# Half-size products for values and gate: the norm factor at the end, its chain in one piece, the squares in other places

## The chip, the core and the metric

The kernel runs on one core of a Trainium2 chip. The core's engines work side by side, each through its own queue, in order: TensorE (PE) does matmuls into PSUM banks, VectorE (DVE) and ScalarE (ACT) do elementwise work, GpSimd (POOL) does some more of it, and SyncE (SP) issues DMAs. Semaphores make one engine wait for another. The metric is the device time of one execution in microseconds (us). The profile shows one execution, from its first to its last instruction (the span).

## What is computed

```python
h = rmsnorm(x, g_mix)                       # x is (1, 512, 1024) float32
z = h @ w_in
q_r, k_r, v_r, gt_r, q_f, k_f, v_f, f_f, a_r, a_f = split_cols(z)
y_r = W_ro( silu(gt_r) * GroupNorm( Retention(rot(q_r), rot(k_r), v_r) ) )
y_f = W_fo( ForgettingAttention(rmsnorm(q_f), rmsnorm(k_f), v_f, log_sigmoid(f_f + b_forget)) )
x = x + W_out( sigmoid(a_r) * y_r + sigmoid(a_f) * y_f )
x = x + SwiGLU(rmsnorm(x))
```

`rmsnorm` multiplies each token's row by `rsqrt(mean(x*x) + 1e-6)`, one number per token, and each column by a gain. The kernel puts the gain into `x` before the products. The number per token, `rstd1`, can be multiplied in behind a product, because a product works on each token's row alone. This case is about the place where that is done for `v_r` (the values) and `gt_r` (the gate).

## The kernel before

**Precision.** Every float32 operand of a matmul is split in two: a leading part (a cast, on ACT) and the remainder (a subtraction, on DVE). `split_raw` (lines 150 to 156) does so for a weight tile of 128 x 1024, `x_sum` (lines 318 to 329) for a sum of blocks of `x`. Three matmuls stand for one product. Weight parts have three buffers (`WB`), so a cast waits until PE has used the tile three places before it.

**Values and gate.** Both have 512 columns. For pairs of blocks the kernel doesn't do eight block products but seven, of sums of blocks (lines 361 to 405). This text calls them products 1 to 7, in order of their calls of `products`:

| product | weights | `x` | banks | adds to |
|---|---|---|---|---|
| 1 | `B11` | `A11` | `x_` | new |
| 2 | `t1` = `B11 + B12` | `s1` = `A21 - A22` | `z_` | new |
| 3 | `B11 + B12 + B22` | `s2` = `s1 - A11` | `x_` | product 1 |
| 4 | `B21` | `A12` | `y_` | new |
| 5 | `t3` = `B12 + B22` | `s3` = `A11 - A21` | `x_` | product 3 |
| 6 | `B22` | `s4` = `s2 + A12` | `z_` | product 2 |
| 7 | `B11 + B12 + B22 + B21` | `A22` | `x_` | product 5 |

Each is 4 blocks of rows x 2 banks x 3 = 24 matmuls of 512 columns. The weight blocks are added in place, so an addition to `B11` waits until the sum before it is split. Product 7 goes bank by bank, the others change banks at every block. Where a product adds to banks that another one filled, the partial sum is first copied out of PSUM into a quarter of `us`. The values `vr` and the gate `gs` come from these quarters and the last banks.

**The norm factor.** Four squares on ACT, with `accum_out`, give the sums `ss1` from `xs`, the token-major copy of `x`, which a DMA brings (line 226). `rsqrt` (lines 109 to 124) makes `rstd1` from them by twelve small instructions on DVE, each depending on the one before. `us` lies in the space of `xs`. The copies out of PSUM (lines 374, 379, 383, 391), the evacuation of the earlier product of `q_r` and `k_r` from the banks `sc` and `tp` to `rz` (lines 375 and 376) and the last steps of `vr` and `gs` all multiply by `rstd1`. Product 4 writes to the `sc` banks.

**Behind the products.** `broadcast_cols` (lines 240 to 250, called in line 410) turns `rstd1` into rows for the gates: with a tile `wide` it makes one broadcast copy on DVE and then four turns on PE, without it four small products into `rb`, which has two buffers, each with a turn. GpSimd rotates `q_r` and `k_r` (`ret_rotate`); its first instruction is made to wait for the last remainder of `t3` (`t3_low`). Then pieces of the retention alternate on PE with the steps of other products, which `fill(RF[...])` places by their cost in us (lines 661 to 686); one step of `w_qf` has three matmuls. The last step for each token tile evacuates `qf` and writes `fz` (line 548) from the same bank. `ret_norm` takes statistics (`bn_stats`, line 501).

**Order.** A planner places each engine's instructions in the order of the code as they come ready. PE's order is pinned between the lines that set `pinned[0]`. `after(a, b)` adds an edge: `a` comes behind `b` on their engine. The norm chain is put behind `t1`'s last remainder (`behind=t1_low`, line 371).

Of the kernel before, what the change touches and what calls it, by code (L numbers as in the profile page):

```python
# [9 lines left out]
F32 = mybir.dt.float32  # L10
F32R = mybir.dt.float32r
I32 = mybir.dt.int32
BF16 = mybir.dt.bfloat16
AF = mybir.ActivationFunctionType
ALU = mybir.AluOpType
AX = mybir.AxisListType

P = 128
D = 1024
S = 512  # L20
NT = S // P
NK = D // P
RH, RDK, RDV = 4, 64, 128
FH, FD = 8, 64
# [10 lines left out]
C_BF = C_GFFN + NK  # L35
# [18 lines left out]
def block_kernel(ctx: ExitStack, tc, x, xT, c_early, c_tab, c_late, w_qf, w_tok, w_vg, w_a, w_y, w_o, w_gu, w_dn, w_dh, out):  # L54
    nc = tc.nc
    PS = bass.MemoryType.PSUM
    tt, ts, stt = nc.vector.tensor_tensor, nc.vector.tensor_scalar, nc.vector.scalar_tensor_tensor
    act = nc.scalar.activation
    pinned = [False, None]

    def after(ins, prev):

        tc.add_manual_dep(ins.ins, prev.ins.name, mybir.DependencyInfo(mybir.DependencyClass.NoSync, mybir.DependencyReason.DATA), reason="order")
# [27 lines left out]
    def bank(tag):  # L91
        return ps.tile([P, 512], F32, name=tag, tag=tag, bufs={"acc": 4, "sc": 2, "tp": 2}[tag])
# [6 lines left out]
    r1 = cst.tile([P, S], F32, name="r1")  # L99
# [9 lines left out]
    def rsqrt(dst, ss, inv_n, shape, nm, pool=None, behind=None):  # L109

        v = (pool or sm).tile(shape, F32, name=nm + "v", tag=nm + "v", bufs=1 if pool else 2)
        yi = (pool or sm).tile(shape, I32, name=nm + "y", tag=nm + "y", bufs=1 if pool else 2)
        a = (pool or sm).tile(shape, F32, name=nm + "a", tag=nm + "a", bufs=1 if pool else 2)
        y = yi.bitcast(F32)
        first = ts(out=v, in0=ss, scalar1=inv_n, scalar2=EPS, op0=ALU.mult, op1=ALU.add)
        if behind is not None:
            after(first, behind)
        ts(out=yi, in0=v.bitcast(I32), scalar1=1, scalar2=None, op0=ALU.logical_shift_right)
        ts(out=yi, in0=yi, scalar1=-1.0, scalar2=float(0x5F3759DF), op0=ALU.mult, op1=ALU.add)
        for i in range(3):  # L120
            stt(out=a, in0=y, scalar=-0.5, in1=y, op0=ALU.mult, op1=ALU.mult)
            tt(out=a, in0=a, in1=v, op=ALU.mult)
            last = stt(out=dst if i == 2 else y, in0=a, scalar=1.5, in1=y, op0=ALU.add, op1=ALU.mult)
        return last
# [6 lines left out]
    WU, WP = 1056, 1152  # L131
    RAW, WB, SG, PT, PR, TB, CBUF = 2, 3, 12, 2, 4, 2, 2
    PREP = [3, 5]
    RF, CF, PF, SF, LAG = (5.32, 4.64, 5.6, 4.6, 11.2), (3.0, 2.0, 2.26, 4.0), 5.9, (0.63, 0.83, 1.57, 1.4), 3
    VF = 1.8

    raw_pools, part_pools, turns = [wp] * RAW, [wp] * WB, [0, 0]
# [163 lines left out]
    def evac_to(dst, func):  # L301
        def f(t, c, acc):
            act(out=dst[:, t, :], in_=acc, func=func, scale=rstd1[:, t:t + 1])
        return f
# [13 lines left out]
    def x_sum(n, p, q, op, behind=None):  # L318

        for i in range(2):  # L320
            to = sums[:, n, 2 * i:2 * i + 2, :]
            p_, q_ = (to if b is None else xv[i][:, :, b[0], b[1]:b[1] + HS] for b in (p, q))
            one = tt(out=to, in0=p_, in1=q_, op=op)
            if behind is not None:
                after(one, behind)
        h = bp.tile([P, 4, HS], F32R, name="sh", tag="sh", bufs=2)
        l = bp.tile([P, 4, HS], F32R, name="sl", tag="sl", bufs=2)
        split_to_parts(sums[:, n], h, l)
        return lambda j, tp: tuple(f[:, j, tp * P:(tp + 1) * P] for f in (h, l))
# [5 lines left out]
    def x_block(b):  # L335
        return lambda j, tp: tuple(f[:, 2 * j + b[0], b[1] + tp * P:b[1] + (tp + 1) * P] for f in (xh, xl))

    def halves_of(block, add=None, behind=None):

        parts = []  # L340
        for v in range(2):
            if add is not None:
                one = tt(out=block[:, v, :], in0=block[:, v, :], in1=add[:, v, :], op=ALU.add)
                if behind is not None:
                    after(one, behind)
            parts.append(split_raw(block[:, v, :]))
        return parts

    def products(os, parts, stat, new, by_bank=False):
        steps = [(j, tp) for j in range(4) for tp in range(2)]  # L350
        for j, tp in sorted(steps, key=lambda s: s[1]) if by_bank else steps:
            h, l = parts[j // 2]
            cs = slice(j % 2 * 512, j % 2 * 512 + 512)
            sh, sl = stat(j, tp)
            for n, (a, b) in enumerate(((sh, h), (sl, h), (sh, l))):
                mm(os[tp], lhsT=a, rhs=b[:, cs], start=new and j + n == 0, stop=j == 3 and n == 2, skip_group_check=not new)

    def scaled(o, bank_, t):
        act(out=o, in_=bank_, func=AF.Copy, scale=rstd1[:, t:t + 1])

    z_ = [bank("acc") for _ in range(2)]
    x_ = [bank("acc") for _ in range(2)]
    pinned[0] = True
    b11 = halves_of(B11)
    products(x_, b11, x_block(A11), True)
    s1, t1 = x_sum(0, A21, A22, ALU.subtract), halves_of(B11, B12, split_raw.last[1])
    for t in range(NT):
        junk = ftok.tile([P, D], BF16, name="junk", tag="sq", bufs=1)
        after(act(out=junk, in_=xs[t // 2][:, t % 2, :], func=AF.Square, accum_out=ss1[:, t:t + 1]), split_raw.last[0])
    t1_low = split_raw.last[1]  # L370
    r_last = rsqrt(rstd1, ss1, 1.0 / D, [P, NT], "n1", behind=t1_low)
    us = [ftok.tile([P, 4, 512], F32, name="u", tag=n) for n in ("qf", "kf")]
    for tp in range(2):
        scaled(us[tp][:, 0, :], x_[tp], tp)
    for t in range(NT):
        evac_to(rz, AF.Copy)(t, 0, accs[t])
    products(z_, t1, s1, True)
    for tp in range(2):
        scaled(us[tp][:, 3, :], z_[tp], tp + 2)
    s2 = x_sum(0, None, A11, ALU.subtract)  # L380
    products(x_, halves_of(B11, B22), s2, False)
    for tp in range(2):
        scaled(us[tp][:, 1, :], x_[tp], tp)
    y_ = [bank("sc") for _ in range(2)]
    products(y_, halves_of(B21), x_block(A12), True)
    s3 = x_sum(1, A11, A21, ALU.subtract, t1_low)
    t3 = halves_of(B12, B22, t1_low)
    t3_low = split_raw.last[1]
    products(x_, t3, s3, False)
    for tp in range(2):  # L390
        scaled(us[tp][:, 2, :], x_[tp], tp + 2)
    s4 = x_sum(0, None, A12, ALU.add, r_last)
    vr = rtok.tile([P, NT, 512], F32, name="vr", tag="rtok0")
    gs = rtok.tile([P, NT, 512], F32, name="gs", tag="rtok1")
    for tp in range(2):
        stt(out=vr[:, tp, :], in0=y_[tp], scalar=rstd1[:, tp:tp + 1], in1=us[tp][:, 0, :], op0=ALU.mult, op1=ALU.add)
    products(z_, halves_of(B22), s4, False)
    for tp in range(2):
        tt(out=gs[:, tp + 2, :], in0=us[tp][:, 3, :], in1=us[tp][:, 2, :], op=ALU.subtract)
        act(out=gs[:, tp + 2, :], in_=gs[:, tp + 2, :], func=AF.Silu)  # L400
        stt(out=gs[:, tp, :], in0=z_[tp], scalar=rstd1[:, tp:tp + 1], in1=us[tp][:, 1, :], op0=ALU.mult, op1=ALU.subtract)
        act(out=gs[:, tp, :], in_=gs[:, tp, :], func=AF.Silu)
    products(x_, halves_of(B11, B21, r_last), x_block(A22), False, by_bank=True)
    for tp in range(2):
        scaled(vr[:, tp + 2, :], x_[tp], tp + 2)
    pinned[0] = False
    bp.release()
    orp = tc.alloc_tile_pool(name="orp", bufs=1, side="right")
    sgp = tc.alloc_tile_pool(name="sgp", bufs=1, side="right")
    broadcast_cols(rstd1, r1)  # L410


    orh = orp.tile([P, RH, S], F32R, name="orh")
# [5 lines left out]
    xiT = cl[:, C_XI:C_LATE].rearrange("p (a q) -> p a q", a=2)  # L419
    gp = nc.gpsimd  # L420
    ret = [{} for _ in range(NT)]

    def ret_rotate(t):
        z5 = rz[:, t, :].rearrange("p (a h s d) -> p a h s d", a=2, h=RH, s=2)
# [69 lines left out]
    def ret_norm(t):  # L494
        o = ret[t]["o"]
        o = [o[h % 2][:, (h // 2) * P:(h // 2 + 1) * P] for h in range(RH)]
        mv = sm.tile([P, RH, 2], F32, name="mv", tag="mv")
        bs = sm.tile([P, RH, 6], F32, name="bs", tag="bs")
        r4 = sm.tile([P, RH], F32, name="r4", tag="r4")
        for h in range(RH):  # L500
            nc.vector.bn_stats(out=bs[:, h, :], in_=o[h])
            nc.vector.bn_aggr(out=mv[:, h, :], in_=bs[:, h, :])  # L502
        rsqrt(r4, mv[:, :, 1], 1.0, [P, RH], "n4")
        og = rwk.tile([P, 512], F32, name="og", tag="og")
        for h in range(RH):
            hs = slice(h * P, (h + 1) * P)
            ts(out=og[:, hs], in0=o[h], scalar1=mv[:, h, 0:1], scalar2=r4[:, h:h + 1], op0=ALU.subtract, op1=ALU.mult)
        ret[t].update(og=og)
# [35 lines left out]
    def evac_qf(t, c, acc):  # L544
        sc = rstd1[:, t:t + 1]
        act(out=qf[:, t, c * 256:c * 256 + 256], in_=acc[:, 0:256], func=AF.Copy, scale=sc)
        if c:
            stt(out=fz[:, t, :], in0=acc[:, 256:264], scalar=sc, in1=ce[:, C_BF:C_BF + FH], op0=ALU.mult, op1=ALU.add)
            qnorm(t)

    def evac_kf(t, c, acc):
# [7 lines left out]
        return cb  # L559

    ra, rb = slice(0, FD), slice(FD, P)
    fox = {}

    def fox_prep(a, part):

# [615 lines left out]
```

## Time and profile before

| what | value |
|---|---|
| median of three runs | 723.43 us (723.15 to 724.76) |
| the profiled execution | 722.19 us |
| its span | 720.4 us |
| mean granted clock of PE | 0.995 |
| DVE busy, 33.86 to 44.63 us | 10.56 of 10.77 us |
| DVE busy, 49.12 to 62.30 us | 7.79 of 13.18 us |
| GpSimd busy, 57.69 to 75.41 us | 16.93 of 17.72 us |

The page gives each engine's busy time and its share of the span. A line of the list of waits has the waiting engine, its tile and line, the releaser, the us in total, how often, and the longest. A row of the timeline has start, duration, engine, line and operation; what stands in square brackets is the idle time of the engine before it, with the releaser. A grouped row has the busy time, the mean duration in ns, and the idle time before. A row of the windows has the window, its length, the busy time with the number of instructions, the clock granted to PE (1.00 is full), the share of the DMA engines and GB/s. A row of the DMA issues ends with KB and the us from issue to landing.

### The profile page before, as it was taken

To read this page: it belongs to the slowest core of one execution; us is meant where nothing else is said; L and a number is where in the kernel's file an instruction comes from. 1 tells how busy PE (TensorE), PEld (TensorE's weight loads), DVE (VectorE), ACT (ScalarE), POOL (GpSimd) and SP (SyncE) were. 2 spreads that over 40 slices of the span, in tenths; PEclk is the share of its full clock that TensorE was granted. 3 is DMA by queue.
4 is the path that set the end of the run, shared out by engine and by line. 5 is a ranking of instruction groups with operands and counts; after the bars stand their busy time and mean duration, and the time that the engine had idled before them with its cause. 6 is when DMAs were issued, how large, how long until landed. Compare 5 with 4: busy or idle time off the path is not lost.

```text
span 720.4 us, 10869 instructions
## 1 busy us (share of the span) xinstructions
PE 703.4 (98%) x4283; PEld 618.4 (86%) x4283; DVE 541.6 (75%) x876; ACT 363.5 (50%) x556; POOL 75.1 (10%) x90
## 2 busy tenths in 40 slices
PE   8969899999999999999999999999999999999998
PEld 6848888888877767888888999999999998888998
DVE  6978558756687786637868788899889998844684
ACT  6666343432576666324644655555655555532251
POOL 0007823011021130000220000000000000000000
PEclk9989999999999999999999999999999999999999
DMA  8900312222322221236503133323332214343112
GB/s 280 417 8 1 119 59 89 88 64 97 112 81 74 89 74 58 89 112 232 211 0 117 60 117 118 102 75 118 117 117 68 110 38 139 117 164 99 62 70 76
DMA packets 19907, 76.33 MB, mean 106 GB/s; under 512 B 2312, under 2 KB 2952, under 8 KB 16656
## 3 DMA queue, kind: packets, MB, share of 16 engines
q1 hardware_dynamic: 19712, 75.62, 31.0%
q8 instruction: 33, 0.54, 0.3%
q14 instruction: 18, 0.15, 0.1%
q10 hardware_dynamic: 144, 0.02, 0.0%
HBM read 73.52 MB, written 2.11 MB: 105 GB/s over the span
## 4 chain that ended last, share of the span: by engine, by line
PE 88%; DVE 5%; ACT 3%; issue 2%; POOL 1%; DMA 1%; SPq 0%; ACTq 0%; DVEq 0%
PE acc L72 55%; PE sc L72 27%; PE tp L72 5%; PE tp L75 1%; DVE pr L607 1%; DVE wl L155 1%; POOL cb L599 1%; ACT wh L154 1%; ACT pr L609 1%; ACT tk L574 1%; DMA raw<-in_w_tok_dram 1%; ACT tk L573 1%; DVE kl L576 1%; DVE pr L611 0%; ACT tq L584 0%
## 5 line engine op out<-in xcount | busy, mean ns | idle before, releaser
L154 ACT CAST wh<-raw 128x1024 fp32r<-128x1024 f32 (+1 forms) x44 | 46.2, 1050 | 93.9 <-PE acc L72 84.7
L72 PE MATMUL sc<-xfh,cl 128*128 128x256 f32 x288 | 83.2, 289 | 0.0
L72 PE MATMUL sc<-xfh,ch 128*128 128x256 f32 x288 | 81.6, 283 | 0.0
L72 PE MATMUL sc<-xfl,ch 128*128 128x256 f32 x288 | 81.4, 283 | 0.0
L155 DVE TENSOR_TENSOR wl<-raw,wh 128x1024 fp32r<-128x1024 f32 (+1 forms) x44 | 56.3, 1280 | 26.1 <-ACT wh L154 26.1
L848 DVE TENSOR_TENSOR cl<-t,ch 128x1024 fp32r<-128x1024 f32 x48 | 58.7, 1222 | 13.7 <-ACT ch L848 13.6
L72 PE MATMUL acc<-xfh,ah 128*128 128x256 f32 (+1 forms) x216 | 63.9, 296 | 0.0
L72 PE MATMUL acc<-xfh,al 128*128 128x256 f32 (+1 forms) x216 | 63.7, 295 | 0.0
L72 PE MATMUL acc<-xfl,ah 128*128 128x256 f32 (+1 forms) x216 | 63.7, 295 | 0.0
L848 ACT CAST ch<-t 128x1024 fp32r<-128x1024 f32 x48 | 50.5, 1052 | 12.8 <-PE tp L72 8.0
L72 PEld LDWEIGHTS sc<-xfh,cl 128*128 128x128 f32 x288 | 55.0, 191 | 0.8 <-DVE cl L848 0.2
L72 PEld LDWEIGHTS sc<-xfh,ch 128*128 128x128 f32 x288 | 55.1, 191 | 0.3 <-ACT u L909 0.2
L72 PEld LDWEIGHTS sc<-xfl,ch 128*128 128x128 f32 x288 | 55.1, 191 | 0.0
L72 PE MATMUL acc<-xh,wh 128*128 128x512 f32 x128 | 52.4, 410 | 0.0
L72 PE MATMUL acc<-wh,xh 128*128 128x512 f32 (+2 forms) x144 | 50.5, 351 | 0.8 <-DVE mv L502 0.8
L72 PE MATMUL acc<-xh,wl 128*128 128x512 f32 x128 | 50.1, 392 | 0.0
L72 PE MATMUL acc<-xl,wh 128*128 128x512 f32 x128 | 49.9, 390 | 0.0
L72 PE MATMUL acc<-wl,xh 128*128 128x512 f32 (+2 forms) x144 | 49.4, 343 | 0.0
L72 PE MATMUL acc<-wh,xl 128*128 128x512 f32 (+2 forms) x144 | 49.4, 343 | 0.0
L848 DVE TENSOR_TENSOR al<-raw,ah 128x1536 fp32r<-128x1536 f32 x24 | 42.2, 1757 | 6.9 <-ACT ah L848 6.9
L72 PEld LDWEIGHTS acc<-xfh,al 128*128 128x128 f32 x216 | 41.3, 191 | 1.0
L72 PEld LDWEIGHTS acc<-xfl,ah 128*128 128x128 f32 x216 | 41.3, 191 | 0.9
(313 smaller groups left out, 1916.2 us busy)
## 6 DMA issues: line engine op xcount, KB each, us to landing
raw<-in_w_gu_dram SPq DMA_DIRECT2D x21, 1024.0 KB, 4.7
raw<-in_w_a_dram SPq DMA_DIRECT2D x16, 512.0 KB, 3.5
t<-in_w_dn_dram SPq DMA_DIRECT2D x14, 512.0 KB, 3.6
blk<-in_w_vg_dram SPq DMA_DIRECT2D x8, 512.0 KB, 10.0
raw<-in_w_tok_dram SPq DMA_DIRECT2D x8, 512.0 KB, 3.5
raw<-in_w_y_dram SPq DMA_DIRECT2D x8, 512.0 KB, 3.5
raw<-in_w_o_dram SPq DMA_DIRECT2D x8, 512.0 KB, 3.6
raw<-in_w_dh_dram SPq DMA_DIRECT2D x4, 1024.0 KB, 4.9
```

The lines of the kernel that those rows point to most:

```text
L72: in_order(nc.tensor.matmul(o, **kw))
L75: in_order(nc.tensor.transpose(out=o, in_=src, identity=ident))
L154: split_raw.last = (nc.scalar.copy(out=h[:, :width], in_=raw[:, :width]), tt(out=l[:, :width], in0=raw[:, :width], in1=f32(h)[:, :width], ...
L155: tt(out=l[:, :width], in0=raw[:, :width], in1=f32(h)[:, :width], op=ALU.subtract))
L573: act(out=tk[e][r], in_=pk[r], func=AF.Copy, scale=gk[r])
L574: act(out=tk[e][o], in_=pk[r], func=AF.Copy, scale=gk[r])
L576: stt(out=kl[e][r], in0=pk[r], scalar=gk[r], in1=f32(tk[e])[r], op0=ALU.mult, op1=ALU.subtract)
L599: gp.tensor_tensor(out=cb[:, qs], in0=cb[:, qs], in1=mask, op=ALU.add)
L607: nc.vector.tensor_tensor_reduce(out=pr[:, :n], in0=cb[:, :n], in1=sc[:, :n], scale=-1.0, scalar=3e38, op0=ALU.add, op1=ALU.min, accum_out=nm)
L609: fox["last"] = act(out=pr[:, :n], in_=pr[:, :n], func=AF.Exp, scale=-1.0, bias=nm, accum_out=rs)
L848: split_to.last = nc.scalar.copy(out=h, in_=src), tt(out=l, in0=src, in1=f32(h), op=ALU.subtract)
```

## The change

It does five things.

1. The copies out of PSUM don't multiply by `rstd1` any more. `vr` is scaled in place on ACT behind its last addition, and `gs` in its Silu.
2. The four squares move: two behind the cast of `B11`'s second half, two between the casts of `t1`'s halves.
3. The norm chain comes behind `t1`'s last remainder as before, and the remainders of the third weight sum and its second addition come behind the chain. The block additions of `t1` and of product 3 are written out half by half. The sums for `s3` and `t3` come behind the remainders of product 3's weights.
4. `broadcast_cols` gets a tile `wide`.
5. `RF[0]` grows from 5.32 to 5.72, and `bn_stats` comes behind the last `fz` traced by then.

```diff
-    RF, CF, PF, SF, LAG = (5.32, 4.64, 5.6, 4.6, 11.2), (3.0, 2.0, 2.26, 4.0), 5.9, (0.63, 0.83, 1.57, 1.4), 3
+    RF, CF, PF, SF, LAG = (5.72, 4.64, 5.6, 4.6, 11.2), (3.0, 2.0, 2.26, 4.0), 5.9, (0.63, 0.83, 1.57, 1.4), 3
...
+    def squares(t, behind):
+        junk = ftok.tile([P, D], BF16, name="junk", tag="sq", bufs=1)
+        one = act(out=junk, in_=xs[t // 2][:, t % 2, :], func=AF.Square, accum_out=ss1[:, t:t + 1])
+        after(one, behind)
+        return one
+
+    def add_to(block, v, other, behind=None):
+        one = tt(out=block[:, v, :], in0=block[:, v, :], in1=other[:, v, :], op=ALU.add)
+        if behind is not None:
+            after(one, behind)
+
     z_ = [bank("acc") for _ in range(2)]
     x_ = [bank("acc") for _ in range(2)]
     pinned[0] = True
-    b11 = halves_of(B11)
-    products(x_, b11, x_block(A11), True)
-    s1, t1 = x_sum(0, A21, A22, ALU.subtract), halves_of(B11, B12, split_raw.last[1])
-    for t in range(NT):
-        junk = ftok.tile([P, D], BF16, name="junk", tag="sq", bufs=1)
-        after(act(out=junk, in_=xs[t // 2][:, t % 2, :], func=AF.Square, accum_out=ss1[:, t:t + 1]), split_raw.last[0])
+    products(x_, halves_of(B11), x_block(A11), True)
+    s1 = x_sum(0, A21, A22, ALU.subtract)
+    sq = squares(1, squares(0, split_raw.last[0]))
+    b11_low = split_raw.last[1]
+    add_to(B11, 0, B12)
+    add_to(B11, 1, B12, b11_low)
+    t1 = [split_raw(B11[:, 0, :])]
+    after(split_raw.last[0], sq)
+    sq = squares(3, squares(2, split_raw.last[0]))
+    t1.append(split_raw(B11[:, 1, :]))
+    after(split_raw.last[0], sq)
     t1_low = split_raw.last[1]
-    r_last = rsqrt(rstd1, ss1, 1.0 / D, [P, NT], "n1", behind=t1_low)
     us = [ftok.tile([P, 4, 512], F32, name="u", tag=n) for n in ("qf", "kf")]
     for tp in range(2):
-        scaled(us[tp][:, 0, :], x_[tp], tp)
+        nc.scalar.copy(out=us[tp][:, 0, :], in_=x_[tp])
+    products(z_, t1, s1, True)
+    s2 = x_sum(0, None, A11, ALU.subtract)
+    r_last = rsqrt(rstd1, ss1, 1.0 / D, [P, NT], "n1", behind=t1_low)
+    add_to(B11, 0, B22)
+    b3 = [split_raw(B11[:, 0, :])]
+    after(split_raw.last[1], r_last)
+    add_to(B11, 1, B22, r_last)
+    b3.append(split_raw(B11[:, 1, :]))
+    b3_low = split_raw.last[1]
+    for tp in range(2):
+        after(nc.scalar.copy(out=us[tp][:, 3, :], in_=z_[tp]), split_raw.last[0])
     for t in range(NT):
         evac_to(rz, AF.Copy)(t, 0, accs[t])
-    products(z_, t1, s1, True)
+    products(x_, b3, s2, False)
     for tp in range(2):
-        scaled(us[tp][:, 3, :], z_[tp], tp + 2)
-    s2 = x_sum(0, None, A11, ALU.subtract)
-    products(x_, halves_of(B11, B22), s2, False)
-    for tp in range(2):
-        scaled(us[tp][:, 1, :], x_[tp], tp)
+        nc.scalar.copy(out=us[tp][:, 1, :], in_=x_[tp])
...
-    s3 = x_sum(1, A11, A21, ALU.subtract, t1_low)
-    t3 = halves_of(B12, B22, t1_low)
+    s3 = x_sum(1, A11, A21, ALU.subtract, b3_low)
+    t3 = halves_of(B12, B22, b3_low)
...
-        scaled(us[tp][:, 2, :], x_[tp], tp + 2)
+        nc.scalar.copy(out=us[tp][:, 2, :], in_=x_[tp])
     s4 = x_sum(0, None, A12, ALU.add, r_last)
+    wide = ftok.tile([P, NT, P], F32, name="wide", tag="sq", bufs=1)
...
-        stt(out=vr[:, tp, :], in0=y_[tp], scalar=rstd1[:, tp:tp + 1], in1=us[tp][:, 0, :], op0=ALU.mult, op1=ALU.add)
+        tt(out=vr[:, tp, :], in0=y_[tp], in1=us[tp][:, 0, :], op=ALU.add)
+        scaled(vr[:, tp, :], vr[:, tp, :], tp)
     products(z_, halves_of(B22), s4, False)
     for tp in range(2):
         tt(out=gs[:, tp + 2, :], in0=us[tp][:, 3, :], in1=us[tp][:, 2, :], op=ALU.subtract)
-        act(out=gs[:, tp + 2, :], in_=gs[:, tp + 2, :], func=AF.Silu)
-        stt(out=gs[:, tp, :], in0=z_[tp], scalar=rstd1[:, tp:tp + 1], in1=us[tp][:, 1, :], op0=ALU.mult, op1=ALU.subtract)
-        act(out=gs[:, tp, :], in_=gs[:, tp, :], func=AF.Silu)
-    products(x_, halves_of(B11, B21, r_last), x_block(A22), False, by_bank=True)
+        evac_to(gs, AF.Silu)(tp + 2, 0, gs[:, tp + 2, :])
+        tt(out=gs[:, tp, :], in0=z_[tp], in1=us[tp][:, 1, :], op=ALU.subtract)
+        evac_to(gs, AF.Silu)(tp, 0, gs[:, tp, :])
+    b7 = halves_of(B11, B21, r_last)
+    products(x_, b7, x_block(A22), False, by_bank=True)
...
-    broadcast_cols(rstd1, r1)
+    broadcast_cols(rstd1, r1, wide)
...
-            nc.vector.bn_stats(out=bs[:, h, :], in_=o[h])
+            first = nc.vector.bn_stats(out=bs[:, h, :], in_=o[h])
+            if "fz" in fox:
+                after(first, fox["fz"])
...
-            stt(out=fz[:, t, :], in0=acc[:, 256:264], scalar=sc, in1=ce[:, C_BF:C_BF + FH], op0=ALU.mult, op1=ALU.add)
+            fox["fz"] = stt(out=fz[:, t, :], in0=acc[:, 256:264], scalar=sc, in1=ce[:, C_BF:C_BF + FH], op0=ALU.mult, op1=ALU.add)
```

More of the change, by code (lines that the diff above doesn't have):

```diff
@@ L421, in block_kernel @@
     ret = [{} for _ in range(NT)]
+    fox = {}
     def ret_rotate(t):
@@ L561, in block_kernel @@
     ra, rb = slice(0, FD), slice(FD, P)
-    fox = {}
     def fox_prep(a, part):
```

## The prediction

> **What bounds the kernel now.** I read the page's busy line first, then the list of what TensorE (PE) waited for, then windows cut at the seven half-size products (lines 361 to 405), then the chain of waits and the timelines inside those windows.
>
> ```profile
> PE 703.4 (98%) x4283; PEld 618.4 (86%) x4283; DVE 541.6 (75%) x876; ACT 363.5 (50%) x556; POOL 75.1 (10%) x90
> ```
>
> PE is busy for all but 17 of 720.4 us, so only what lets PE wait less can count. The list of PE's waits has three entries on lines that the diff touches:
>
> ```profile
> PE acc L72 <- ACT u L359: 6.6, 1, 6.6
> PE tp L75 <- DVE rb L248: 2.0, 2, 1.1
> ...
> PE acc L72 <- DVE mv L502: 0.8, 1, 0.8
> ```
>
> The windows (span, PE busy, granted clock, DMA share, GB/s) show the first of them in place: products 1 and 2, the hole, product 3, product 7, the broadcast behind it, and everything behind 160 us.
>
> ```profile
> 27.82:38.87 11.05, 11.04 (x49) 1.00 0.78 320
> 38.87:45.49 6.62, 0.00 (x1) 0.75 0.00 0
> 45.49:52.71 7.22, 7.22 (x24) 0.75 0.00 0
> ...
> 69.03:74.47 5.44, 5.44 (x25) 1.00 0.16 37
> 74.47:78.06 3.59, 1.62 (x12) 1.00 0.66 220
> ...
> 160.00:720.40 560.40, 554.89 (x3485) 1.00 0.30 100
> ```
>
> A product takes 5.44 us. Product 3 stands behind a hole of 6.62 us and then takes 7.22 us, because the granted clock fell during the hole. The chain of waits says what the hole is:
>
> ```profile
> 43.56 0.17 DVE n1a L121
> ...
> 44.55 0.17 DVE rstd L123
> 44.72 0.02 issue
> 44.75 0.70 ACT u L359
> ```
>
> Product 3 adds into the banks of product 1, so product 1's partial sum must be copied out first. That copy (line 374) multiplies by `rstd1`, the end of the norm chain. So PE starts again at 45.49, behind a factor that the product doesn't need.
>
> **The change, term by term.**
>
> *Term 1, the hole.* Lines 374, 379, 383 and 391 become plain copies, and the factor comes later (`scaled` on `vr`, and the scale of the Silu). Product 1 ends at 33.26 (27.82 + 5.44), its copies can end by about 34.7, and product 3 can follow product 2 at 38.70. The seven products then take 7 x 5.44 = 38.08 us; now they take 74.47 - 27.82 = 46.65. Removed: **8.57 us** (6.62 of hole, 1.78 of low clock, 0.17 of the last matmul's tail).
>
> What is late next? First the squares. They must end before the copies, which reuse the space of `xs`. I read when `xs` lands and what ACT does meanwhile:
>
> ```profile
> 15.20 1.14 SPq L226 DMA_DIRECT2D xs<-in_x_dram  x2
> ```
> ```profile
> xs<-in_x_dram SPq DMA_DIRECT2D x1, 1024.0 KB, 10.0
> ```
> ```profile
> xs<-in_x_dram SPq DMA_DIRECT2D x1, 1024.0 KB, 11.7
> ```
> ```profile
> 28.02 1.06 ACT L154 CAST wh<-blk 128x1024 fp32r<-128x1024 f32 x1 [3.74 <-PE tp L72]
> ...
> 30.57 1.06 ACT L154 CAST wh<-blk 128x1024 fp32r<-128x1024 f32 x1 [0.15 <-PE acc L72]
> 31.53 1.05 ACT L369 ACTIVATE junk<-xs 128x1024 bf16<-128x1024 f32 x1
> 32.49 0.18 ACT L369 ACTIVATION_READ_ACCUMULATOR junk<-xs 128x1 f32 x1
> ```
>
> A square with the read of its sum takes 1.14 us (31.53 to 32.67). The first half of `xs` lands at 25.2, so squares 0 and 1 fit from 25.2 to 27.5 into the 3.74 us that ACT sits idle ahead of 28.02, and cost nothing. The second half, issued near 16, lands at 27.7. Squares 2 and 3 come behind the cast at 28.02 and end near 31.3, which pushes the cast of 30.57 back by 0.75 us. Its result serves the second half of product 2 at 33.26 + 2.72 = 35.98. Cast and remainder (1.06 + 1.22) end before 33.9: hidden. If `xs` landed over 2 us later, that cover would be gone.
>
> Then the chain. Its steps depend on each other and start 0.20 us apart (43.56 to 44.55 is five steps). Twelve in one piece are 2.4 us, from 33.86, where `t1`'s last remainder ends, to 36.3. So `rstd1` comes at 36.3 instead of 44.7. Product 4 writes the `sc` banks, whose evacuation to `rz` still needs the factor. It starts at 44.14:
>
> ```profile
> 45.90 1.27 ACT L303 ACTIVATE rz<-sc,rstd 128x512 f32<-128x512 f32 x2
> ```
>
> Four evacuations at this pace are 2.5 us. ACT has a free stretch after 36.3 until the next cast near 38.5, so they end near 38.8. If they stand behind the casts and copies instead, they end near 43.4, still before 44.14. I take nothing for them.
>
> *Term 2, the norm factor's broadcast.* Two of its four turns now stop PE, because `rb` has two buffers:
>
> ```profile
> 76.75 0.33 PE L75 MATMUL tp<-ctab,rb 128*128 128x128 f32 x1 [1.07 <-DVE rb L248]
> 77.97 0.33 PE L75 MATMUL tp<-ctab,rb 128*128 128x128 f32 x1 [0.90 <-DVE rb L248]
> ```
>
> The change makes one copy into `wide`, which can run any time after the chain, so all four turns find their data. Removed: 1.07 + 0.90 = **1.97 us**. The trace has no such broadcast copy; it is bounded by zero and by four slow `rb` writes (1.3 each), and I take the nearest row, a cast of 512 columns at 0.42.
>
> *Term 3, the order of `bn_stats` and `fz`.*
>
> ```profile
> 107.73 0.19 DVE L548 SCALAR_TENSOR_TENSOR fz<-acc,rstd,ce 128x8 f32<-128x8 f32 x1
> ```
> ```profile
> 104.62 0.39 PE L72 MATMUL acc<-wh,xh 128*128 128x264 f32 x1
> ...
> 108.07 0.47 PE L72 MATMUL acc<-wh,xh 128*128 128x512 f32 x1 [0.76 <-DVE mv L502]
> ```
>
> PE waits for the bank that the last `fz` reads, and this `fz` stands among the statistics (the row that ended the wait is one of theirs). Its matmuls (104.62) come after that piece of retention on PE. The larger first RF lets one more step (0.32 by MM3) go ahead of it, so all four `fz` exist when `ret_norm` is traced, and the new edge puts the statistics behind them. Removed: **0.76 us**. The step is moved, not added.
>
> *Term 4, what DVE must now do without the hole.* This is the term that costs. Without the hole PE comes 8.57 us earlier for the same work on VectorE (DVE). Durations, from the grouped rows of 19 to 57 us and of 57 to 76 us:
>
> ```profile
> L155 DVE TENSOR_TENSOR wl<-blk,wh 128x1024 fp32r<-128x1024 f32 x10 | 12.2, 1220 | 3.5 <-ACT wh L154 3.5
> ...
> L323 DVE TENSOR_TENSOR sums<-xf 128x512 f32<-128x512 f32 x4 | 2.7, 687 | 0.0
> ```
> ```profile
> L155 DVE TENSOR_TENSOR wl<-blk,wh 128x1024 fp32r<-128x1024 f32 x5 | 7.6, 1529 | 2.3 <-ACT wh L154 2.2
> ```
> ```profile
> 57.85 0.74 POOL L432 TENSOR_TENSOR ta<-rz,cl 128x256 f32<-128x256 f32 x1 [10.21 <-DVE wl L155]
> ```
>
> Neighbours overlap by 0.08, so a large operation is 1.14 and a half one 0.61. From 33.86 to the last remainder that product 7 needs: the chain 2.4; ten remainders of weights 11.4; five block additions 5.7; four half sums 2.4; two remainders of sums 2.3; two writes of `vr` 1.2; two of `gs` 1.2; `wide` 0.4. Together 27.0 us. Product 7 starts at 60.46 and reaches its second half of weights at 61.82, their remainder at 62.3: 28.4 us are there. So DVE has 1.4 us to spare if nothing slows it. But GpSimd starts rotating once `t3`'s remainder is done (row 57.85; then near 50), and beside it the same operation takes 1.53 instead of 1.22, a quarter more. On the work behind 50 (a remainder of `t3` 1.14, that of the `s4` sums 1.14, `vr` 1.2, `B22` 2.3, `gs` 1.2, `B11`'s last addition and two remainders 3.4: some 10 us) that is 2.4 us: short by **1.0 us**, which I take as new waits. The lower bound is 0 (no slowing). The upper bound takes the slowest ratio, that of the row of 1.78 against 1.22, on all 10 us: 4.6 - 1.4 = 3.2.
>
> ```profile
> 68.25 1.78 DVE L155 TENSOR_TENSOR wl<-blk,wh 128x1024 fp32r<-128x1024 f32 x1 [0.72 <-ACT wh L154]
> ```
>
> The two extra `scaled` on ACT (0.7 each, as row 44.75) fall between casts that wait for PE: nothing. No DMA is added; loads behind the products are released earlier with PE.
>
> **Sum.** 8.57 + 1.97 + 0.76 - 1.0 = 10.3 us. The profiled execution took 722.19 (span 720.4, 1.8 around it): 711.9. The median of the three runs is 1.24 above that execution; from it, 723.43 - 10.3 = **713.1 us**. Behind 78 us PE is bound by its own matmuls almost everywhere (554.89 of 560 us behind 160), so what is gained early should arrive at the end.
>
> **The rivals.**
>
> *A smaller hole stays in front of product 3 or 4.* On ACT, if the copies, then the four evacuations, then the cast of `B21` run in that order behind the cast of `B11`'s second half (ending near 39.7), `B21` is cast by 44.4 and its remainder is done at 45.5, against 44.6 wanted (two matmuls behind 44.14): 0.9 us. If DVE also slips two large operations in front of `B11`'s second half (2.3, against a reserve of 1.0): 1.3 more. With term 4 the gain is 10.3 - 2.2 = 8.1: 715.3. For it speaks that DVE mixed such operations into the chain before; against it, the new edges. 0.17.
>
> *GpSimd blocks DVE outright.* If each of ten operations behind 50 us waits for one GpSimd operation of 0.74, that is 7.4 - 1.4 = 6.0 us: 723.43 - 11.3 + 6.0 = 718.1. Against it: the five remainders there were longer by 0.31 in the mean (1.53 against 1.22), not by 0.74. 0.07. The Trainium skill ("SBUF — State Buffer", Who interferes with whom) says that a VectorE instruction with two SBUF inputs and a GpSimd one that reads SBUF exclude each other for a whole instruction; by that rule the sum is this rival's. The mean of 1.53 fits a wait behind a part of the operations only.
>
> *DVE becomes the bound and PE's clock falls again (slower).* If products 4 to 7 each wait 1.3 us on DVE and lose 1.78 to the clock as product 3 did, that is 4 x 3.08 = 12.3 against 11.3 gained: 724.4. It decides once DVE needs over 8.3 us per product; one with two additions, two weight remainders, two sums and their remainder needs 7.0, slowed by a quarter 8.7. But only product 5 has all that behind the hole, and a wait of 1.07 left the clock at 1.00 (window 74.47). 0.03.
>
> *It doesn't do what it says:* the chain stays late, `rstd1` at 44.7 as now, and product 4 waits for the `sc` banks (to 45.5 instead of 44.14) in place of product 3: 1.4 lost, 714.5, inside the range. 0.05.
>
> **How the numbers follow.** The forecast has 0.68. Its own range runs from 710.9 (no new waits, 712.1, and an execution as much below the median as the profiled one) to 715.3 (new waits of 3.2). I take 710.9 to 717.0, which holds the smaller hole and half of the way to the blocking rival. About 0.2% (1.4 us) is what can be told from no change. Faster needs a gain over 1.4 us: all but the slower rival and mishaps unseen: 0.94; same 0.03; slower 0.03.
>
> **What would show it.** The copies of `u` near 33.5 without waiting for `rstd`; the seven products within 39 to 40 us of 27.8, at clock 1.00; no PE wait on `rb`; no wait of PE near 96 us on the statistics. New PE waits on DVE in products 5 to 7 would be term 4. A clock under 1.00 behind 28 us, or a PE wait over 2 us there, makes the forecast wrong.

## The result and the profile after

The changed kernel takes 716.78 us (median of six executions, 715.89 to 720.65); the kernel before 722.78 in the same measurements. The ratio is 0.9923, with a 95% interval of 0.9896 to 0.9951: faster by 0.8%, where 1.4% was forecast. On the prediction's base that is 723.43 x 0.9923 = 717.9 us, just above its range. Ratios leave out one execution of e7, which took 1784 us where its seven others took 720 to 723 us; the record doesn't show why. The changed kernel's profiled execution took 715.89 us with a span of 714.1, so 6.3 us less than the span of before.

The busy line of the page and the list of what PE waited for, from the changed kernel's profile:

```profile
PE 702.2 (98%) x4283; PEld 617.0 (86%) x4283; DVE 539.6 (76%) x873; ACT 363.8 (51%) x558; POOL 73.8 (10%) x90
```

```profile
PE tp L75 <- ACT pT L653: 2.1, 4, 0.8
PE acc L72 <- DVE wl L155: 1.7, 3, 0.7
PE acc L72 <- ACT wh L154: 1.6, 1, 1.6
```

PE's busy time is that of before less 1.2 us; the rest of the gain is idle time. The three waits of before that the diff aimed at are gone: none on `u`, none on `rb`, none on `mv`. In their place stand waits for weight parts, on DVE (`wl`) and ACT (`wh`); those on `pT` were there before (1.8 us). The windows show where. They are cut, as before, at products 1 and 2, then 3, 4, 5, 6, 7, and the first matmuls of `w_qf` (columns: window, length, PE busy, clock, DMA share, GB/s):

```profile
28.16:39.04 10.88, 10.88 (x50) 1.00 0.71 291
39.04:45.09 6.05, 5.74 (x26) 1.00 0.00 0
45.09:50.52 5.43, 5.43 (x25) 1.00 0.00 0
50.52:56.95 6.43, 5.74 (x25) 1.00 0.02 4
56.95:62.39 5.44, 5.44 (x25) 1.00 0.00 0
62.39:70.93 8.54, 6.21 (x25) 1.00 0.12 16
70.93:73.87 2.94, 2.94 (x26) 1.00 0.66 220
```

Products 1, 2, 4 and 6 take 5.44 us each. Products 3, 5 and 7 are 0.61, 0.99 and 3.10 us too long. The idle time on PE in them is 0.31, 0.69 and 1.62 + 0.71 us; the last two, from PE's timeline:

```profile
65.72 0.50 PE L72 MATMUL acc<-wh,xh 128*128 128x512 f32 x1 [1.62 <-ACT wh L154]
67.17 0.50 PE L72 MATMUL acc<-wl,xh 128*128 128x512 f32 x1 [0.71 <-DVE wl L155]
```

Each stop costs some 0.3 more until the matmuls follow each other at the old pace. The seven products take 70.93 - 28.16 = 42.77 us against 46.65 before and 38.08 without a stop. So of the 8.57 us of the hole, 3.88 arrived and 4.69 were given back.

DVE's timeline in the same stretch shows who made PE wait (start, duration, instruction):

```profile
57.23 1.76 DVE L343 TENSOR_TENSOR blk<-blk,blk 128x1024 f32<-128x1024 f32 x1
58.91 2.25 DVE L423 TENSOR_TENSOR gs<-u 128x512 f32<-128x512 f32 x2
61.08 1.75 DVE L155 TENSOR_TENSOR wl<-blk,wh 128x1024 fp32r<-128x1024 f32 x1
62.76 1.75 DVE L343 TENSOR_TENSOR blk<-blk,blk 128x1024 f32<-128x1024 f32 x1
64.43 0.94 DVE L244 COPY wide<-rstd 128x512 f32<-128x512 f32 x1
65.30 0.68 DVE L425 TENSOR_TENSOR gs<-acc,u 128x512 f32<-128x512 f32 x1
65.90 1.21 DVE L155 TENSOR_TENSOR wl<-blk,wh 128x1024 fp32r<-128x1024 f32 x1
```

There is no idle time in these rows. The addition at 62.76 makes the second half of product 7's weights; ACT casts it at 64.62, and the remainder at 65.90 is what PE waits for last. The large operations but the last take 1.75 us where they took 1.22 ahead of GpSimd's work, and GpSimd is busy for 12.72 of the 13.11 us from 54.00 to 67.11.

### The profile page after: what moved, and what is told of

It is laid out like the page before. It is cut to its first block, busy times and chain, and to the rows that moved or that the text cites. A ratio compares the mean times of both kernels' runs of the same rounds, so it can differ in the third digit from the quotient of the medians.

```text
span 714.1 us, 10865 instructions
## 1 busy us (share of the span) xinstructions
PE 702.2 (98%) x4283; PEld 617.0 (86%) x4283; DVE 539.6 (76%) x873; ACT 363.8 (51%) x558; POOL 73.8 (10%) x90
## 4 chain that ended last, share of the span: by engine, by line
PE 84%; DVE 8%; ACT 3%; issue 3%; DMA 1%; POOL 0%; SPq 0%; DVEq 0%; ACTq 0%; POOLq 0%
PE acc L72 54%; PE sc L72 25%; PE tp L72 3%; PE tp L75 2%; DVE wl L155 2%; DVE pr L634 1%; DMA xf<-in_xT_dram 1%; DVE blk L343 1%; DVE sums L323 1%; DVE blk L368 1%; ACT wh L154 1%; ACT pr L636 1%; DVE xl L198 0%; ACT junk L363 0%; DMA cb<-cd 0%
## 5 line engine op out<-in xcount | busy, mean ns | idle before, releaser
L875 DVE TENSOR_TENSOR cl<-t,ch 128x1024 fp32r<-128x1024 f32 x48 | 58.6, 1222 | 13.7 <-ACT ch L875 13.6
```

The lines of the kernel that those rows point to most:

```text
L875: split_to.last = nc.scalar.copy(out=h, in_=src), tt(out=l, in0=src, in1=f32(h), op=ALU.subtract)
```

## The experiments

**Theory A:** VectorE is the bound of products 3 to 7, because GpSimd's rotation beside it lengthens its operations. **Theory B:** the order on VectorE is at fault, since other work stands in front of product 7's weights. The first four runs tell them apart; the next three take the change's parts alone; the last ones look at what was left.

### e1, the changed kernel again

> The changed kernel once more, as the base that the next three are measured against on the same chip. All theories: 6 us under the kernel before, with PE waits of some 3.3 us in products 3 to 7.

717.5 us, ratio 0.9937 (0.9915 to 0.9958). The waits are where they were, but the executions spread: 716.0, 717.4, 717.5, 718.0 and 720.2, at mean clocks of 1.0, 0.997, 1.0, 0.997 and 0.995. The profiled one was the slowest. Its windows behind 60 us (columns as above), with product 7 starting at 63.88:

```profile
65.50:67.20 1.70, 0.08 (x1) 1.00 0.00 0
67.20:68.70 1.50, 0.95 (x3) 0.63 0.00 0
68.70:70.70 2.00, 2.00 (x5) 0.50 0.00 0
...
74.40:76.00 1.60, 1.60 (x12) 0.99 0.00 0
```

The clock falls to half right behind a wait of 1.64 us and stays there for some 7 us (67.6 to 74.4). In the profile shown first, the same wait (1.62) left the clock at 1.00. So the same two waits make product 7 3.1 us too long in one execution (8.54) and 5.8 in another (11.22).

### e2, the rotation later

```diff
     b7 = halves_of(B11, B21, r_last)
+    b7_low = split_raw.last[1]
...
+        tb_first = gp.tensor_tensor(out=tb, in0=z2, in1=s, op=ALU.mult)
         if t == 0:
-            tc.add_manual_dep(first.ins, t3_low.ins.name, ...)
-        gp.tensor_tensor(out=tb, in0=z2, in1=s, op=ALU.mult)
+            for one in (first, tb_first):
+                tc.add_manual_dep(one.ins, b7_low.ins.name, ...)
```

(and an added edge keeps GpSimd's products for `gs` behind the second rotation, where the changed kernel has them)

> GpSimd's rotation starts behind the last weight remainder of product 7 instead of t3's. Theory A (GpSimd beside VectorE slows VectorE's two-input operations from 1.22 to 1.75 us, 4.6 us over products 3 to 7, and VectorE is the bound there): these operations take 1.22 again, PE's waits in the products fall from 3.3 to under 1 us, and the time falls by 3 to 4.5 us against e1. Theory B (the order on VectorE is at fault: the subtractions for gs and the copy to wide stand in front of product 7's weights): the wait of 1.62 us stays, and the time falls by under 1 us. If the rotation is then late for its turn on PE, a new wait there gives it back.

712.5 us (711.94 to 712.7), ratio 0.9861 (0.9845 to 0.9878): 5.0 us under e1's median, above the 3 to 4.5 expected; three of e1's five executions had also lost to the clock. Grouped rows of DVE (busy us, mean ns, idle before), first of the changed kernel between 53 and 65.9 us:

```profile
L155 DVE TENSOR_TENSOR wl<-blk,wh 128x1024 fp32r<-128x1024 f32 x3 | 5.0, 1703 | 0.0
L343 DVE TENSOR_TENSOR blk<-blk,blk 128x1024 f32<-128x1024 f32 x2 | 3.5, 1755 | 0.0
L423 DVE TENSOR_TENSOR gs<-u 128x512 f32<-128x512 f32 x2 | 2.2, 1162 | 0.0
L419 DVE TENSOR_TENSOR vr<-sc,u 128x512 f32<-128x512 f32 x2 | 1.3, 684 | 0.0
L244 DVE COPY wide<-rstd 128x512 f32<-128x512 f32 x1 | 0.9, 945 | 0.0
```

and of e2 between 50 and 66 us:

```profile
L155 DVE TENSOR_TENSOR wl<-blk,wh 128x1024 fp32r<-128x1024 f32 x6 | 7.2, 1222 | 0.1
L343 DVE TENSOR_TENSOR blk<-blk,blk 128x1024 f32<-128x1024 f32 x2 | 2.4, 1219 | 0.0
...
L423 DVE TENSOR_TENSOR gs<-u 128x512 f32<-128x512 f32 x2 | 1.3, 685 | 0.0
L419 DVE TENSOR_TENSOR vr<-sc,u 128x512 f32<-128x512 f32 x2 | 1.3, 686 | 0.0
...
L244 DVE COPY wide<-rstd 128x512 f32<-128x512 f32 x1 | 0.4, 420 | 0.0
```

With GpSimd quiet, the rows fall back to their old length; `vr`, which takes one input from PSUM, never grew. The waits of products 3 and 7 are gone, and only the 0.67 at the start of product 5 is left. GpSimd's rotation, now from 63.4 us on, made nobody on PE wait, and the four executions all had a clock of 1.0. The seven products take 39.16 us (row under e9) against 42.77: the slowing cost PE 3.61 of the 4.69 us. The other 1.08 us are product 5's wait and its restart, which GpSimd doesn't cause. Theory A holds, but for product 5.

### e3 and e4, another order on VectorE

```diff
+    b7 = halves_of(B11, B21, r_last)
+    b7_low = split_raw.last[1]
     for tp in range(2):
-        tt(out=gs[:, tp + 2, :], in0=us[tp][:, 3, :], in1=us[tp][:, 2, :], op=ALU.subtract)
+        after(tt(out=gs[:, tp + 2, :], in0=us[tp][:, 3, :], in1=us[tp][:, 2, :], op=ALU.subtract), b7_low)
...
-        tt(out=gs[:, tp, :], in0=z_[tp], in1=us[tp][:, 1, :], op=ALU.subtract)
+        after(tt(out=gs[:, tp, :], in0=z_[tp], in1=us[tp][:, 1, :], op=ALU.subtract), b7_low)
...
-    b7 = halves_of(B11, B21, r_last)
...
-    broadcast_cols(rstd1, r1, wide)
+    broadcast_cols(rstd1, r1, wide, b7_low)
```

(the last argument puts the copy to `wide` behind `b7_low`)

> VectorE does product 7's additions and remainders ahead of the subtractions for gs and the copy to wide; GpSimd as in e1. Theory B: 2.25 + 0.94 + 0.68 = 3.9 us go from in front of product 7's last remainder, so its waits of 1.62 and 0.71 go: 3 us under e1, while those of products 3 and 5 (0.31, 0.69) stay. Theory A in its pure form: the operations stay at 1.75, but the same reordering should help too, as the queue in front is shorter; what tells the theories apart is the duration of the operations here and the result of e2.

> e2 and e3 together. Theory A: nothing beyond e2 but for the rest of its waits (under 1 us); theory B: nothing beyond e3. If both causes are needed to fill the queue, each alone removes most of the waits and together they leave at most the one in product 3.

e3: 714.25 us, ratio 0.9885 (0.9867 to 0.9903). Product 7 ran without a wait; those of products 3 (0.21 + 0.53) and 5 (0.70) stayed. The weight remainders there still took 1.54 us in the mean (e2: 1.22). The same row as in e2's groups, from 50 to 66 us of e3:

```profile
L155 DVE TENSOR_TENSOR wl<-blk,wh 128x1024 fp32r<-128x1024 f32 x6 | 9.0, 1535 | 0.0
```

So the order is a second way to the same end: it shortens the queue in front of the weights, but not the operations. e4: 713.78 us, ratio 0.9881 (0.9862 to 0.9900). Both together bring nothing beyond e2; the one wait left in the products is that of product 5 (0.69). So the wait in product 7, the largest, needed both causes: slow operations, and other work ahead of its weights. Taking away either removes it. The slowing alone explains the wait in product 3, which e3 keeps and e2 loses.

### e5, `wide` alone

```diff
+    wide = ftok.tile([P, NT, P], F32, name="wide", tag="sq", bufs=1)
...
-    broadcast_cols(rstd1, r1)
+    broadcast_cols(rstd1, r1, wide)
```

on the kernel before.

> The kernel before with the tile wide alone. If the two waits on rb are all that this part is worth: 2.0 us plus two restarts of PE (some 0.3 each), so 2.0 to 2.6 us under the kernel before. If the split of w_qf's weights is next in line there, under 1 us.

721.75 us, ratio 0.9991 (0.9981 to 1.0001): 0.6 us by the medians, at most 1.4 by the interval, which also holds no change; not 2. Its waits of PE on `rb` are gone, but another took their place (columns of the timeline, first PE, then ACT):

```profile
77.71 0.39 PE L72 MATMUL acc<-wh,xh 128*128 128x256 f32 x1 [1.70 <-ACT vr L359]
```
```profile
76.00 1.07 ACT L154 CAST wh<-raw 128x1056 fp32r<-128x1056 f32 x1 [1.95 <-DMA raw<-in_w_qf_dram]
76.98 0.68 ACT L359 ACTIVATE vr<-acc,rstd 128x512 f32<-128x512 f32 x1
```

PE wants the bank of the last part of `vr`. Its evacuation was ready behind product 7, but on ACT it stands behind a cast that waits for a DMA. In the changed kernel the planner put the evacuation (71.13) ahead of that cast (72.65), and the stretch behind the products fell from 5.34 us to 2.94; in e5 it fell to 4.90.

### e6, the statistics and the first RF alone

The diff is part 5 of the change, on the kernel before.

> The kernel before with the longer first RF and the statistics behind fz alone. The wait of 0.76 us goes: 0.8 to 1.1 us gained until 160 us. The changed kernel loses 0.7 us again between 200 and 270 us. If the longer RF does that, by other places of the fill steps in the attention, the loss is here too and the whole is worth 0.1 to 0.4 us; if not, it stays at 0.8 to 1.1.

722.24 us, ratio 0.9997 (0.9981 to 1.0014): no difference. The windows tell why. Those of the kernel before, from the second group of products to the attention and through the attention:

```profile
110.91:201.03 90.12, 90.12 (x461) 1.00 0.30 94
201.03:277.80 76.77, 74.42 (x403) 1.00 0.22 69
```

and of e6, cut at the same matmuls:

```profile
109.64:199.72 90.08, 90.08 (x462) 1.00 0.29 94
199.72:277.11 77.39, 73.95 (x403) 1.00 0.21 69
```

It is 1.27 us ahead at the first cut, 1.31 at the second, 0.69 at the third. Of the first 1.27 us, 0.31 were there before the changed lines came into play (product 3 starts at 45.18, in the kernel before at 45.49), so this part gains 0.96. Then the attention takes 0.62 us longer, as the fill steps in it moved.

### e7, the copies alone

The lines of part 1 of the change, on the kernel before; squares, chain, additions and statistics as they were.

> The kernel before with the factor at the end alone: squares, chain, additions, wide and statistics as before. If the copies' wait on the factor is the whole of the hole, as in the prediction's term 1, the chain may stay in pieces and this alone brings most of 8.57 us less the waits on VectorE (some 4 us). If the sc banks, whose evacuation still needs the factor, are next, the hole moves in front of product 4, stays over 3.4 us long and takes the clock with it: 2 to 4 us gained, with a PE wait on rz or u of 3 to 5 us at 44 us.

720.45 us (the median of all eight), ratio 0.9973 (0.9957 to 0.9988). Windows at products 1 and 2, 3 with the wait behind it, 4, and 5 to 7:

```profile
29.39:40.27 10.88, 10.88 (x50) 1.00 0.63 259
40.27:49.01 8.74, 5.60 (x25) 1.00 0.00 0
49.01:56.20 7.19, 7.19 (x25) 0.76 0.01 3
56.20:72.52 16.32, 16.32 (x74) 1.00 0.10 31
```

Product 3 starts without a wait, and the hole moves in front of product 4: 3.14 us until `rz` has left the `sc` banks, and the clock falls. The chain of waits shows the end of the norm's chain, with a large operation between its last steps (start, us, what):

```profile
44.83 1.14 DVE wl L155
...
46.94 1.22 DVE wl L155
48.16 0.09 DVE rstd L123
48.25 0.02 issue
48.27 0.70 ACT rz L303
```

With the factor out of the copies, the chain came even later: 18.9 us behind the start of product 1, against 16.9 in the kernel before. The two remainders shown stand between its steps; counted in order, those two came at 51.03 and 53.89 in the kernel before, behind the hole. So the copies alone don't bring the gain: something of parts 2 and 3 (the squares, the chain in one piece, the order behind it) is needed with them. No run takes these apart; that the chain in one piece is what counts is argued from the rows. Products 5 to 7 need 16.32 us, exactly three times 5.44: with a hole ahead of them VectorE isn't the bound.

### e8 and e9, the order at the start of product 5

```diff
     s4 = x_sum(0, None, A12, ALU.add, r_last)
+    after(x_sum.low, t3_low)
```

on e2 (`x_sum.low` is the remainder of the sum).

> e2 with the remainder of the s4 sums put behind t3's remainders on VectorE. If the wait of 0.69 us in front of product 5 is only that one operation of 1.14 us in the queue, it goes: 0.7 to 1.0 us under e2, near 711.6. If VectorE is the bound as a whole even without GpSimd, a wait of the same size comes up in product 6 or 7 and the time stays.

712.28 us, ratio 0.9860 (0.9838 to 0.9883), with a wait of 0.70 in the old place: inconclusive, because the planner moved one of product 7's additions into the place that came free. e9 puts those additions and `wide` behind `t3` too:

```diff
-    b7 = halves_of(B11, B21, r_last)
+    b7 = halves_of(B11, B21, t3_low)
...
-    broadcast_cols(rstd1, r1, wide)
+    broadcast_cols(rstd1, r1, wide, t3_low)
```

> e2 with the remainder of the s4 sums, product 7's additions and the copy to wide all put behind t3's remainders on VectorE (in e8 the planner put another large operation, an addition for product 7, into the freed place, so e8 didn't test it). If the wait of 0.69 us in front of product 5 is one large operation too much in the queue, product 5 starts without a wait, and PE's products 3 to 7 take 38.1 to 38.6 us; 0.7 to 1.0 us under e2. If VectorE is the bound as a whole even without GpSimd beside it, the wait comes up again in product 6 or 7 and the time stays at e2's.

711.85 us, ratio 0.9862 (0.9843 to 0.9882). Product 5 starts without a wait; one of 0.32 comes up in product 7. The seven products, e2 first, then e9:

```profile
28.28:67.44 39.16, 38.49 (x169) 1.00 0.23 88
```
```profile
27.89:66.53 38.64, 38.32 (x170) 1.00 0.24 94
```

38.64 us are 0.56 above the 38.08 without a stop, where e2 was 1.08 above. So about half of what product 5's wait cost was order. The rest came up again in product 7, as it would if VectorE had too much work; no run tests that. Against e2 the times can't tell it from no change.

### e10 and e11, the fill steps put back

```diff
-    RF, CF, PF, SF, LAG = (5.72, 4.64, 5.6, 4.6, 11.2), ...
+    RF, CF, PF, SF, LAG = (5.72, 4.64, 5.6, 4.6, 10.8), ...
```

on e2, and in e11 on e9.

> e2 with the last RF at 10.8 instead of 11.2, so that the fill steps of the attention stand where the kernel before has them, while the retention keeps the longer first RF. If the 0.7 us that e6 lost again between 200 and 270 us come from the places of these steps, they are gained: 0.5 to 0.8 us under e2, with PE's gain at 280 us as large as at 200. If they come from something else, no change.

> e2, e9 and e10 together. If both effects are real and independent: 1.2 to 1.8 us under e2, near 711; every execution at a clock of 1.00, since no wait of PE over 0.5 us is left in products 3 to 7.

The attention in e2 and in e10, cut at the same matmuls:

```profile
190.53:268.12 77.59, 73.97 (x402) 1.00 0.23 69
```
```profile
191.74:268.40 76.66, 74.38 (x402) 1.00 0.22 69
```

The 0.9 us are the fill steps' places. e10 took 712.12 us, ratio 0.9856 (0.9839 to 0.9873), too close to e2 for its time to show this. e11 took 710.7 us (710.32 to 711.04), ratio 0.9838 (0.9823 to 0.9853). It is the fastest version here, 1.6% under the kernel before, twice what the change alone brings. That its two parts add up isn't shown, though. From the start of product 1 to the end of the span its profile takes 681.4 us, that of e10 681.2 and that of e2 682.4. Its seven products take 39.06 us, with waits of 0.20 and 0.39, so little of e9's gain is left there.

## Why the prediction was right or wrong

**Term 1, the hole: right.** No PE wait on `u`, product 3 behind product 2, and the clock at 1.00 in the profile shown first. That the `sc` banks would be free was right too (no wait at product 4), with the whole change; with the copies alone (e7) they became the hole.

**Where it failed: term 4, "new waits", 1.0 us, with a range of 0 to 3.2.** The place and the mechanism were right; the size was 4.69 in the profile shown first, where the seven products took 42.77 us instead of the 39 to 40 announced. The sum for VectorE can be checked against the rows. From the start of the chain (35.05) to the end of product 7's last remainder (67.11) are 32.06 us, against 27.0 predicted. The parts:

- *The slowing beside GpSimd, the main part.* Each of the five large operations from 54.03 to 64.4 us grew by some 0.5 (1703 and 1755 against 1222 and 1219), the two `gs` by 0.48, `wide` by 0.52. With one addition at 38.46, beside GpSimd's first operation, that is 4.55 us of VectorE's time, where 2.4 were taken. e2 takes GpSimd away, and PE gets 3.61 us back. The mean of 1.53 from the trace of before was the wrong price. It is over five remainders. One of them ran ahead of GpSimd's rotation, which started at 57.85, and one took only 1.28 us, having started before GpSimd's next operation (59.49):

```profile
56.55 1.22 DVE L155 TENSOR_TENSOR wl<-blk,wh 128x1024 fp32r<-128x1024 f32 x1
...
59.21 1.28 DVE L155 TENSOR_TENSOR wl<-blk,wh 128x1024 fp32r<-128x1024 f32 x1
```

  The other three took 1.61 to 1.78, and with both engines full such a length was the typical one. So the 4.6 us behind the range's upper end would have been the estimate. That they meet the 4.55 is luck in part: of the 10 us of work, 3.5 (the remainders of `t3` and of the `s4` sums, ahead of GpSimd's rotation, and `vr`) didn't grow, while the addition at 38.46, one more addition for product 7 and `wide` weren't in it and grew. The sum also took `gs` and `wide` to stand ahead of product 7's weights, as they do; e3 shows that another order there takes product 7's wait away at the slow lengths.
- *A third `gs`* came ahead of product 7's last remainder (row 65.30): 0.61.
- *The squares weren't hidden.* The planner put the cast of the `s2` sum, which waited on VectorE, between squares 0 and 1:

```profile
25.50 1.06 ACT L363 ACTIVATE junk<-xs 128x1024 bf16<-128x1024 f32 x1 [1.53 <-DMA xs<-in_x_dram]
...
27.66 1.05 ACT L332 CAST sh<-sums 128x1024 fp32r<-128x1024 f32 x1 [1.01 <-DVE sums L323]
28.61 1.05 ACT L363 ACTIVATE junk<-xs 128x1024 bf16<-128x1024 f32 x1
```

  So `t1`'s casts, and with them the chain, came 0.85 us later than predicted, counted from product 1's start (35.05 - 28.16 against 33.86 - 27.82).

Together 4.55 + 0.61 + 0.85 + 27.0 - 28.4 = 4.6, and 4.69 were lost. The clock, which the forecast priced at nothing, came on top in other executions (e1). Of the six of the result, the three at a mean clock of 1.00 took 715.89 to 716.16 us, the three at 0.995 to 0.998 took 717.41 to 720.65. On the prediction's base the first three come to 723.43 x 715.93 / 722.78 = 716.6 us, just inside the range. So both together passed its upper end.

**Term 2: too small in the whole, too large alone.** 2.40 us in this pair of profiles (5.34 to 2.94; 1.97 plus two restarts), but some 0.6 alone (e5), because the evacuation of `vr` was next in line. It stood behind the cast that waits for a DMA in the kernel before too (77.05, behind 76.08). The prediction asked what hides the copy, and not what else PE wants there.

**Term 3: right at its place, given back later.** 31.10 to 30.06 us between the same matmuls, so 1.04. "The step is moved, not added" missed that the longer RF moves the steps behind it: the attention went from 76.77 to 77.57 us. e6 shows the loss with this part alone, e10 takes it away.

**Sum.** 3.88 + 2.40 + 1.04 - 0.80, and 0.34 lost to a later first product (28.16 against 27.82): 6.2 us of the 6.3 seen in the spans. The first product started between 27.3 and 29.7 us in the profiles of these runs, so single profiles can't be compared to better than 2 us in total, while their windows can.

**The rivals.** The smaller hole in front of product 3 or 4 didn't come, and neither did the late chain; e7 shows what it would have cost. The slower rival named the right pair, a wait on DVE and a falling clock, but in four products: e1 shows it in product 7 alone, behind a wait of 1.64 us. The blocking rival was nearer than its chance of 0.07 said: 4.55 us of slowing against its 7.4. That its 718.1 us lies beside the 717.9 measured is luck in part, since the squares, the third `gs` and the clock weren't in it. The Trainium skill ("SBUF — State Buffer", Who interferes with whom) says that a VectorE operation with two SBUF inputs contends with a GpSimd operation that reads SBUF, that one in a two-port mode, which a copy can enter, contends with GpSimd as well, and that one with at most one SBUF input outside such a mode doesn't. The rows agree: 1222 to 1703 and 420 to 945 ns for the former, 686 and 684 for `vr`. Whether the copy to `wide` runs in such a mode no row here shows.

## What to carry to other kernels

When a wait is taken away, sum up the work of the engine that used the waiting time, up to the deadline behind it, and price it at the length its operations have beside a busy neighbour, not at a mean that mixes in operations which ran without the neighbour. Work that is needed only later (here GpSimd's rotation) is best released behind the rush, not in it. And a part of a change that gains locally can be worth nothing alone: look for the next wait at its place, and for what moves behind it.

## What the runs showed of the hardware

PE's clock fell to 0.50 behind a wait of 1.64 us in one execution and stayed at 1.00 behind 1.62 us in another; behind 3.14 us (e7) it fell as well. The Trainium skill ("TensorE: Matmul & The Clock Gate", Why this matters for your kernels) advises against idle gaps over some 3 us; here a shorter one was enough, and the slow stretch lasted some 7 us. GpSimd is slowed in turn: an operation of its rotation took 0.74 us while VectorE was idle (e2, at 65.92) and up to 1.77 beside VectorE (the changed kernel, at 65.93).
